# Key, query and weight-split pieces moved from GpSimd to VectorE in a two-layer decoder trunk, with square roots begun one work unit later, query copies two units later, and the first norm begun one unit earlier

## Chip, core and metric

The kernel runs on one core of a Trainium2 chip. The metric is device time in microseconds of one execution. The engines are TensorE (PE, with PEld for its weight loads), VectorE (DVE), ScalarE (ACT), GpSimd (POOL) and SyncE (SP), which starts the transfers of weights.

## What is computed

A decoder of two layers on 256 tokens of width 1024, in float32. Each layer is a gated feed-forward block, a mixer with three attention branches, and a second feed-forward block:

```python
for l in range(DEPTH):                                   # DEPTH = 2
    x = x + 0.5 * swiglu_ffn(x, ffn1_norm[l], ffn1_w_gu[l], ffn1_w_down[l])
    h = rms_norm(x, mix_norm[l])
    x = x + hybrid_mixer(h, ...)
    x = x + 0.5 * swiglu_ffn(x, ffn2_norm[l], ffn2_w_gu[l], ffn2_w_down[l])
...
# hybrid_mixer: one projection h @ w_in, split into the inputs of
#   o_a: stick-breaking attention (4 heads)
#   o_b: NSA attention (8 query heads; compressed, selected and window keys)
#   o_c: DSA attention (4 query heads, an indexer picks the top 64 keys)
merged = g_a * (o_a @ w_br_a) + g_b * (o_b @ w_br_b) + g_c * (o_c @ w_br_c)   # g = sigmoid(h @ w_gate)
return merged @ w_out
# queries and keys: rms_norm over 64 columns, then a rotation (rope) of the first 16
```

## The kernel before

**Units.** All weights pass through `unit` (lines 229 to 247). A unit is one 128x1024 (sometimes 128x896) block of weights: SP loads it into one of four `raw` buffers, ACT copies it, rounded, into one of three `wh` buffers (line 242), and DVE, or for the units that the list `slow` names GpSimd, writes the rest `raw - wh` into `wl` (line 244). Two units later (`LA = 2`) PE multiplies with `wh` and `wl`. So a unit's `raw` buffer is free for the next load only when its `wl` is written, and its `wh` buffer only when PE has used it.

**Threads.** Everything else of the mixer (norms, rope, transposes, the indexer's top-k, attention) is written as generators. `tick` (line 209) runs after every unit and advances each generator to its next `yield`; `yield n` means n units later. A scheduler then sets the order of the instructions on DVE, ACT, GpSimd and SP; each engine runs its own list strictly in that order. PE keeps the written order.

**Where the change is.** In the mixer, `norm_rope` (line 665) squares, sums, takes a root with `head_rsqrt` (line 654: one DVE instruction for `u`, then Ln and Exp on ACT, line 501, then three DVE instructions), scales and calls `rope` (line 640). `keys` treats the DSA queries and all keys (`p1`, 9 heads), `queries` the 8 NSA queries (`q8`, two token tiles), `compress` the compressed keys. `stack_k` (line 695) makes a rounded copy and a rest of keys ("L part", line 700); line 790 does the same for the DSA queries. In `indexer` the top-k is 8 rounds of max (line 757) and match-replace (line 758) for each of the two token tiles. `evac` (lines 526 and 528) empties PSUM accumulators (`acc`, three banks) of the input projection. `u`, `y`, `w` of the roots share small buffers, two of each; the root `N["r"]` of the norm ahead of the mixer (line 398) lies in one of the `y` buffers for the whole projection.

**The first norm.** `first_norm` (line 1175) waits two units after its sums and runs `norm_rstd`, which waits `FY2 = 2` more units between its root (line 388) and the product that spreads it (`tp<-dg`, line 413).

Of the kernel before, what the change touches and what calls it, by code (L numbers as in the profile page):

```python
# [112 lines left out]
WB = 2  # L113
WARM = 46
M0 = 7
FY2 = 2
ACC = 3
SC = 2
TP = 2
# [4 lines left out]
def decoder_trunk(ctx: ExitStack, tc: tile.TileContext, x_in, consts, gains, hgain, gu1, dn1, win, wkc, wgate, cw1, cw2,  # L124
# [17 lines left out]
    def nm(s):  # L142
        cnt[0] += 1
        return f"{s}_{cnt[0]}"
# [37 lines left out]
    def psum(tag, bufs):  # L182
        return ps.tile([P, 512], F32, tag=tag, bufs=bufs, name=nm(tag))
# [203 lines left out]

    def rsqrt(src, n, inv):

        u, y, w = (small.tile([P, 32], F32, tag=t, bufs=2, name=nm(t))[:, 0:n] for t in "uyw")  # L390
        V.tensor_scalar(out=u, in0=src, scalar1=inv, scalar2=EPS, op0=ALU.mult, op1=ALU.add)
        V.tensor_scalar(out=y.bitcast(I32), in0=u.bitcast(I32), scalar1=-0.5, scalar2=float(0x5f3759df), op0=ALU.mult,
                        op1=ALU.add)
        for _ in range(3):
            V.tensor_tensor(out=w, in0=y, in1=y, op=ALU.mult)
            V.scalar_tensor_tensor(out=w, in0=w, scalar=-0.5, in1=u, op0=ALU.mult, op1=ALU.mult)
            V.scalar_tensor_tensor(out=y, in0=w, scalar=1.5, in1=y, op0=ALU.add, op1=ALU.mult)
        return y
# [91 lines left out]
    def mixer(l, nrm, nxt):  # L490
# [9 lines left out]
        def act_exp(func=AF.Exp, **kw):  # L500
            e = A.activation(func=func, **kw)  # L501
            nosync(e, table)
            exps.append(e)
# [4 lines left out]
        def st(shape, tag, bufs, n):  # L508
            return small.tile([P] + shape, F32, tag=tag, bufs=bufs, name=nm(n))
# [26 lines left out]
                yield 1  # L536


        gate, iw = st([NT, 24], "gate", 2, "gate"), st([NT, 8], "iw", 2, "iw")
        rq = st([NT], "rq", 2, "rq")  # L540
        p0 = b4("p0")[:, 0:640].rearrange("p (t c) -> p t c", t=NT)
        vds = mt([NT, HD], "vds")
# [97 lines left out]
        def rope(v, nh, half, cs, sn):  # L640

            nt = cs.shape[1]
            sh = [P, nt, nh, 2 * half]
            a = mt([NT, 9, 16], "ra")[:, 0:nt, 0:nh, 0:2 * half]
            b = mt([NT, 9, 16], "rb")[:, 0:nt, 0:nh, 0:2 * half]
            cb = cs.unsqueeze(2).to_broadcast(sh)
            sb = sn.unsqueeze(2).to_broadcast(sh)
            V.tensor_tensor(out=a, in0=v[:, :, :, 0:2 * half], in1=cb, op=ALU.mult)
            G.tensor_tensor(out=b[:, :, :, 0:half], in0=v[:, :, :, half:2 * half], in1=sb[:, :, :, 0:half], op=ALU.mult)  # L649
            V.tensor_tensor(out=b[:, :, :, half:2 * half], in0=v[:, :, :, 0:half], in1=sb[:, :, :, half:2 * half],  # L650
                            op=ALU.mult)
            V.tensor_tensor(out=v[:, :, :, 0:2 * half], in0=a, in1=b, op=ALU.add)

        def head_rsqrt(ss, n):

            u, y, w = (st([32], t, 2, t)[:, 0:n] for t in "uyw")
            V.tensor_scalar(out=u, in0=ss, scalar1=1.0 / HD, scalar2=EPS, op0=ALU.mult, op1=ALU.add)
            act_exp(out=y, in_=u, func=AF.Ln)
            act_exp(out=y, in_=y, scale=-0.5)
            V.tensor_tensor(out=w, in0=y, in1=y, op=ALU.mult)  # L660
            V.scalar_tensor_tensor(out=w, in0=w, scalar=-0.5, in1=u, op0=ALU.mult, op1=ALU.mult)
            V.scalar_tensor_tensor(out=y, in0=w, scalar=1.5, in1=y, op0=ALU.add, op1=ALU.mult)
            return y

        def norm_rope(v, nh, gs, t0=0):

            nt = v.shape[1]
            ss = st([32], "hs", 2, "hs")[:, 0:nt * nh]
            for t in range(nt):
                sq = b4("sq")[:, 0:nh * HD].rearrange("p (h d) -> p h d", d=HD)  # L670
                A.activation(out=sq, in_=v[:, t], func=AF.Square)
                V.tensor_reduce(out=ss[:, t * nh:(t + 1) * nh], in_=sq, axis=AX.X, op=ALU.add)
            yield 1
            r = head_rsqrt(ss, nt * nh).rearrange("p (a b) -> p a b", b=nh)
            yield 1
            V.tensor_tensor(out=v, in0=v, in1=r.unsqueeze(3).to_broadcast([P, nt, nh, HD]), op=ALU.mult)
            for a, n, k in gs:
                g = hg[:, k * HD:(k + 1) * HD].unsqueeze(1).unsqueeze(1)
                V.tensor_tensor(out=v[:, :, a:a + n], in0=v[:, :, a:a + n], in1=g.to_broadcast([P, nt, n, HD]),  # L679
                                op=ALU.mult)  # L680
            yield 1
            rope(v, nh, 8, tab("cs")[:, t0:t0 + nt], tab("sn")[:, t0:t0 + nt])
            yield 0
# [11 lines left out]
        def stack_k(dst, src, nh):  # L695

            d = dst.rearrange("p h (a d) -> p h a d", d=HD)
            b = src.unsqueeze(2).to_broadcast([P, nh, 2, HD])
            A.activation(out=d[:, :, 0:2].bitcast(F32R), in_=b, func=AF.Copy)
            G.tensor_tensor(out=d[:, :, 2:4], in0=b, in1=d[:, :, 0:2], op=ALU.subtract)  # L700

        live = {"E": EB, "PT": 4}
        later = [cc("ncz")[:, S - P * (t + 1):S] for t in range(NT)]
# [68 lines left out]
        def keys():  # L772
# [14 lines left out]
                evens(out=kD[:, :, s], in_=heads(tp))  # L787
            dq = b4("dq").rearrange("p (t h a d) -> p t h a d", t=NT, a=2, d=HD)
            A.activation(out=dq[:, :, :, 0].bitcast(F32R), in_=p1[:, :, 0:4], func=AF.Copy)
            G.tensor_tensor(out=dq[:, :, :, 1], in0=p1[:, :, 0:4], in1=dq[:, :, :, 0], op=ALU.subtract)  # L790
            done.add("kSW")
            yield 1
            for t in range(NT):
# [9 lines left out]
        def compress():  # L803
# [47 lines left out]
            junk = mt([1, 256], "kc4")[:, 0, 0:HD]  # L851
            css = st([1], "css", 2, "css")
            A.activation(out=junk, in_=kc, func=AF.Square, accum_out=css)
            yield 1
            rc = head_rsqrt(css, 1)
            V.scalar_tensor_tensor(out=kc, in0=kc, scalar=rc, in1=hg[:, 5 * HD:6 * HD], op0=ALU.mult, op1=ALU.mult)
            ra, rb = st([16], "cra", 2, "cra"), st([16], "crb", 2, "crb")
            V.tensor_tensor(out=ra, in0=kc[:, 0:16], in1=cc("csc"), op=ALU.mult)
# [15 lines left out]
        def queries():  # L874
            yield from need(4)
            parts = [norm_rope(q8[t][:, :, HD:P].unsqueeze(1), 8, ((0, 8, 3),), t) for t in range(NT)]
            for _ in zip(*parts):
                yield 1
            for t in range(NT):
                A.activation(out=q8[t][:, :, 0:HD].bitcast(F32R), in_=q8[t][:, :, HD:P], func=AF.Copy)  # L880
                V.tensor_tensor(out=q8[t][:, :, HD:P], in0=q8[t][:, :, HD:P], in1=q8[t][:, :, 0:HD], op=ALU.subtract)
            yield 4
            for t in range(NT):
                for h in range(0, 8, 4):
                    tp = transposes([q8[t][:, h + j] for j in range(4)])
                    evens(out=qN[:, h:h + 4, t * P:(t + 1) * P], in_=heads(tp))
                if t == 0:
                    yield 1
            done.add("qN")
# [48 lines left out]
        def dsa():  # L938
            yield from need("mdsa", "qD")
            for t in range(NT):  # L940
# [9 lines left out]
                PT = attn_pt(t, E)  # L950
                live["E"] += 1
                yield 1
                o = psum("tp", TP)
                for b in range(t + 1):
                    for h in range(4):
                        mm(o[h % 2 * HD:(h % 2 + 1) * HD, h // 2 * P:(h // 2 + 1) * P], vds[:, b], PT[h][b],
# [138 lines left out]
        for g in (keys, indexer, queries, nsa_units, compress, stick_breaking, nsa, compressed, dsa):  # L1095
            spawn(g())
        gates = iter(range(12))
        slow.extend(int(u in (10, 14, 18, 27)) for u in range(62))
        for g in ORDER:
            if g == "f":  # L1100
                for kv in range(2):
# [73 lines left out]
    def first_norm():  # L1175
        for m in range(KD):
# [2 lines left out]
                yield 1  # L1179
            if m == 6:  # L1180
                nc.sync.dma_start(out=cst, in_=consts)
        yield 2
        yield from norm_rstd(nrm, FY2)
        yield 4
        V.tensor_scalar(out=negi, in0=ident, scalar1=NEG, scalar2=None, op0=ALU.mult)
# [81 lines left out]
```

## Time and profile before

| | before |
|---|---|
| median of 3 runs | 1226.95 us (1223.9 to 1229.97) |
| profiled execution: time | 1228.48 us |
| its span | 1226.7 us |
| PE busy | 1206.3 us, 98% |
| PEld busy | 1075.5 us, 88% |
| DVE busy | 886.6 us, 72% |
| ACT busy | 697.6 us, 57% |
| POOL busy | 163.4 us, 13% |

Busy shares are means over the whole span. The two mixers lie about 205 to 440 us and 810 to 1045 us into it; the feed-forward blocks fill the rest.

### The profile page before, as it was taken

What the parts mean: (1) busy time and instruction counts of PE and PEld (TensorE: products, weight loads), DVE (VectorE), ACT (ScalarE), POOL (GpSimd) and SP (SyncE); (2) the same over time, 40 slices, a digit from 0 to 9 for tenths busy, and PEclk for the clock granted to TensorE, in tenths of its full rate; (3) what the DMA queues carried; (4) which work ended last, traced back from release to release, by engine and by line L of the source; (5) the groups of instructions that cost most, each with busy time, mean ns of one, the idle gap of its engine ahead of it and who ended that gap; (6) DMA issues with size and microseconds to landing.
All of it is one profiled execution on the core that took longest, in us unless ns stands there. A gap on an engine that the chain in (4) does not pass through costs nothing.

```text
span 1226.7 us, 20872 instructions
## 1 busy us (share of the span) xinstructions
PE 1206.3 (98%) x7878; PEld 1075.5 (88%) x7878; DVE 886.6 (72%) x1563; ACT 697.6 (57%) x1261; POOL 163.4 (13%) x195
## 2 busy tenths in 40 slices
PE   8999999989999999999999999999999999999998
PEld 7888888878989988888888888897798899888887
DVE  7766677896766877766777766778877578776664
ACT  6655555555666565555556555545556745655542
POOL 2111011330000111110111110122300001111100
PEclk9999999999999999999999999999999999999999
DMA  7555566644334565556656655665433346555563
GB/s 265 178 188 184 179 188 193 213 145 131 106 102 141 177 193 191 191 185 182 189 182 196 191 186 184 191 197 192 139 127 112 104 148 195 181 192 190 186 198 104
DMA packets 60885, 212.09 MB, mean 173 GB/s; under 512 B 6992, under 2 KB 8048, under 8 KB 60784
## 3 DMA queue, kind: packets, MB, share of 16 engines
q1 hardware_dynamic: 60192, 209.65, 53.7%
q0 software_dynamic: 448, 1.08, 0.4%
q8 instruction: 62, 1.02, 0.3%
q14 instruction: 39, 0.32, 0.1%
q10 hardware_dynamic: 144, 0.02, 0.0%
HBM read 209.15 MB, written 1.05 MB: 171 GB/s over the span
## 4 chain that ended last, share of the span: by engine, by line
PE 89%; DVE 6%; DMA 2%; ACT 1%; POOL 1%; issue 1%; SPq 0%; ACTq 0%; DVEq 0%; POOLq 0%
PE acc L196 67%; PE sc L196 17%; PE tp L689 2%; DVE wl L244 2%; PE o L196 1%; DMA raw<-in_win 1%; DVE isc L758 1%; PE tp L196 1%; DVE m L757 1%; ACT wh L242 1%; DVE isc L748 1%; DMA gn<-in_gains 0%; POOL rb L649 0%; DVE p L679 0%; DVE isc L746 0%
## 5 line engine op out<-in xcount | busy, mean ns | idle before, releaser
L242 ACT ACTIVATE wh<-raw 128x1024 fp32r<-128x1024 f32 (+4 forms) x402 | 412.1, 1027 | 412.4 <-PE acc L196 285.6
L244 DVE TENSOR_TENSOR wl<-raw,wh 128x1024 fp32r<-128x1024 f32 (+3 forms) x394 | 468.3, 1191 | 221.5 <-ACT wh L242 220.4
L196 PE MATMUL acc<-aT,wh 128*128 128x512 f32 (+1 forms) x1696 | 414.1, 342 | 1.1 <-ACT wh L242 1.1
L196 PEld LDWEIGHTS acc<-aT,wh 128*128 128x128 f32 x1696 | 264.9, 189 | 41.0 <-ACT wh L242 1.5
L196 PE MATMUL acc<-aT,wl 128*128 128x256 f32 x1280 | 297.1, 280 | 0.7 <-DVE wl L244 0.7
L196 PE MATMUL acc<-hT,wh 128*128 128x512 f32 (+1 forms) x792 | 239.1, 369 | 0.0
L196 PEld LDWEIGHTS acc<-aT,wl 128*128 128x128 f32 x1280 | 215.9, 189 | 3.0 <-DVE wl L244 2.0
L196 PE MATMUL sc<-aT,wh 128*128 128x512 f32 x544 | 190.8, 395 | 0.0
L196 PE MATMUL acc<-hT,wl 128*128 128x256 f32 x704 | 186.6, 283 | 0.0
L196 PEld LDWEIGHTS acc<-hT,wh 128*128 128x128 f32 x792 | 137.4, 188 | 26.9
L196 PE MATMUL sc<-aT,wl 128*128 128x256 f32 x544 | 150.6, 278 | 0.0
L196 PEld LDWEIGHTS acc<-hT,wl 128*128 128x128 f32 x704 | 127.1, 188 | 0.0
L442 POOL TENSOR_TENSOR v<-v,R 128x256 f32<-128x256 f32 x88 | 68.2, 779 | 414.3 <-DVE v L358 359.9
L196 PEld LDWEIGHTS sc<-aT,wh 128*128 128x128 f32 x544 | 101.8, 188 | 23.6
L196 PEld LDWEIGHTS sc<-aT,wl 128*128 128x128 f32 x544 | 102.3, 188 | 0.4
L386 POOL TENSOR_TENSOR ssum<-ssum,sq 128x256 f32<-128x256 f32 x42 | 38.3, 912 | 449.1 <-ACT sq L385 448.9
L196 PE MATMUL acc<-wh,aT 128*128 128x512 f32 (+1 forms) x320 | 83.9, 404 | 4.6 <-ACT p L526 4.6
L196 PEld LDWEIGHTS acc<-wh,aT 128*128 128x128 f32 x320 | 59.3, 194 | 15.9 <-ACT p L526 5.5
L357 ACT ACTIVATE half<-acc 128x256 f32<-128x256 f32 x136 | 49.4, 365 | 2.6 <-PE acc L196 1.8
L444 DVE TENSOR_TENSOR v<-v,v 128x256 f32<-128x256 f32 x88 | 38.4, 440 | 12.1 <-ACT v L443 4.3
L376 DVE SCALAR_TENSOR_TENSOR aT<-x,gn,aT 128x256 fp32r<-128x256 f32 x48 | 40.5, 853 | 6.9 <-ACT aT L375 6.9
L501 ACT ACTIVATE E<-sc,mx 128x128 f32<-128x128 f32 (+1 forms) x80 | 32.6, 418 | 21.8 <-DVE mx L905 21.7
(241 smaller groups left out, 1262.8 us busy)
## 6 DMA issues: line engine op xcount, KB each, us to landing
raw<-in_gu SPq DMA_DIRECT2D x175, 512.0 KB, 3.7
raw<-in_dn SPq DMA_DIRECT2D x64, 512.0 KB, 3.5
raw<-in_wgate SPq DMA_DIRECT2D x48, 512.0 KB, 3.4
raw<-in_win SPq DMA_DIRECT2D x32, 512.0 KB, 3.5
raw<-in_dn SPq DMA_DIRECT2D x32, 384.0 KB, 3.0
raw<-in_wbr SPq DMA_DIRECT2D x16, 512.0 KB, 3.4
raw<-in_wout SPq DMA_DIRECT2D x16, 512.0 KB, 3.5
raw<-in_cw SPq DMA_DIRECT2D x8, 512.0 KB, 4.5
```

What stands on the lines that cost most here:

```text
L196: return pe(T.matmul(o, lhsT=lhsT, rhs=rhs, start=start, stop=stop, skip_group_check=True))
L242: A.activation(out=wh[:, w], in_=raw[:, w], func=AF.Copy)
L244: e.tensor_tensor(out=wl[:, w], in0=raw[:, w], in1=wh[:, w].bitcast(F32), op=ALU.subtract)
L357: A.activation(out=t, in_=b[:, S:2 * S], func=AF.Copy)
L376: V.scalar_tensor_tensor(out=dst[:, m, 1], in0=xs[m], scalar=g[:, m:m + 1], in1=dst[:, m, 0].bitcast(F32), op0=ALU.mult, op1=ALU.subtract)
L386: G.tensor_tensor(out=ssum, in0=ssum, in1=sq, op=ALU.add)
L442: G.tensor_tensor(out=g, in0=g, in1=N["R"], op=ALU.mult)
L444: V.tensor_tensor(out=u, in0=u, in1=g, op=ALU.mult)
L501: e = A.activation(func=func, **kw)
L689: pe(T.transpose(tp[:, b * P:(b + 1) * P], src, ident))
L748: V.scalar_tensor_tensor(out=isc[t], in0=rl[:, j], scalar=w, in1=isc[t], op0=ALU.mult, op1=ALU.add)
L757: V.max(out=m8, in_=isc[t])
```

## The change

Several pieces of the mixer change their engine and keep their arithmetic: the first half of `rope`'s second product (line 649), the L part of the keys (`stack_k`, line 700, five calls per layer), the L part of the DSA queries (line 790), and the `wl` of units 10, 14 and 18 go from GpSimd to DVE; unit 27's `wl` stays on GpSimd. `head_rsqrt` becomes a generator: it writes `u`, yields one unit, and then issues Ln and Exp; the yield that stood ahead of it is gone. The root's buffers become three `u`, four `y` and two `w`, of 18 columns instead of 32. `queries` waits two units ahead of its copies (lines 880 and 881) and two behind them, where it waited none and four. The DSA output bank comes from `acc` instead of `tp`. `first_norm` waits one unit less, `FY2` one more. `gate` and `iw` have one buffer.

```diff
-FY2 = 2
+FY2 = 3
...
     def rsqrt(src, n, inv):
-        u, y, w = (small.tile([P, 32], F32, tag=t, bufs=2, name=nm(t))[:, 0:n] for t in "uyw")
+        u, y, w = (small.tile([P, 18], F32, tag=t, bufs={'u': 3, 'y': 4, 'w': 2}[t], name=nm(t))[:, 0:n] for t in "uyw")
...
-            G.tensor_tensor(out=b[:, :, :, 0:half], in0=v[:, :, :, half:2 * half], in1=sb[:, :, :, 0:half], op=ALU.mult)
+            V.tensor_tensor(out=b[:, :, :, 0:half], in0=v[:, :, :, half:2 * half], in1=sb[:, :, :, 0:half], op=ALU.mult)
...
         def head_rsqrt(ss, n):
-            u, y, w = (st([32], t, 2, t)[:, 0:n] for t in "uyw")
+            u, y, w = (st([18], t, {'u': 3, 'y': 4, 'w': 2}[t], t)[:, 0:n] for t in "uyw")
             V.tensor_scalar(out=u, in0=ss, scalar1=1.0 / HD, scalar2=EPS, op0=ALU.mult, op1=ALU.add)
+            yield 1
             act_exp(out=y, in_=u, func=AF.Ln)
...
         def norm_rope(v, nh, gs, t0=0):
...
-            yield 1
-            r = head_rsqrt(ss, nt * nh).rearrange("p (a b) -> p a b", b=nh)
+            r = (yield from head_rsqrt(ss, nt * nh)).rearrange("p (a b) -> p a b", b=nh)
...
-            G.tensor_tensor(out=d[:, :, 2:4], in0=b, in1=d[:, :, 0:2], op=ALU.subtract)
+            V.tensor_tensor(out=d[:, :, 2:4], in0=b, in1=d[:, :, 0:2], op=ALU.subtract)
...
-            G.tensor_tensor(out=dq[:, :, :, 1], in0=p1[:, :, 0:4], in1=dq[:, :, :, 0], op=ALU.subtract)
+            V.tensor_tensor(out=dq[:, :, :, 1], in0=p1[:, :, 0:4], in1=dq[:, :, :, 0], op=ALU.subtract)
...
             for _ in zip(*parts):
                 yield 1
+            yield 2
             for t in range(NT):
...
-            yield 4
+            yield 2
...
-                o = psum("tp", TP)
+                o = psum("acc", ACC)
...
-        slow.extend(int(u in (10, 14, 18, 27)) for u in range(62))
+        slow.extend(int(u == 27) for u in range(62))
...
-        yield 2
+        yield 1
         yield from norm_rstd(nrm, FY2)
```

The scheduler's lists move with it. On DVE, where the second query tile (`q_403`) is turned and copied in the first mixer, the list before reads as follows (`m_642` is the last of the eight top-k rounds, `mdsa` the mask that they give):

```order
L676 TENSOR_TENSOR q_403_2154<-q_403_2154,y_2870 128x8x64
L652 TENSOR_TENSOR q_402_2153<-ra_2956,rb_2957 128x8x16
L679 TENSOR_TENSOR q_403_2154<-q_403_2154,hg_2139 128x8x64
L244 TENSOR_TENSOR wl_3034<-raw_3031,wh_3033 128x1024
L648 TENSOR_TENSOR ra_2962<-q_403_2154,cst 128x128
L650 TENSOR_TENSOR rb_2963<-q_403_2154,cst 128x8x8
L881 TENSOR_TENSOR q_402_2153<-q_402_2153 128x8x64
L652 TENSOR_TENSOR q_403_2154<-ra_2962,rb_2963 128x8x16
L758 MATCH_REPLACE isc_2376<-m_642_3313,isc_2376 128x256
L763 SCALAR_TENSOR_TENSOR mdsa_3316<-isc_2375,cst 128x128
L244 TENSOR_TENSOR wl_3069<-raw_3066,wh_3068 128x1024
L881 TENSOR_TENSOR q_403_2154<-q_403_2154 128x8x64
```

and now, from the same turn of `q_403` to its copy (`m_587` and `m_588` are the fourth round, `m_598` and `m_599` the fifth):

```order
L652 TENSOR_TENSOR q_403_2154<-ra_2962,rb_2963 128x8x16
L758 MATCH_REPLACE isc_2375<-m_587_2993,isc_2375 128x128
L757 MAX m_588_2996<-isc_2376 128x8
L244 TENSOR_TENSOR wl_3002<-raw_2999,wh_3001 128x1024
L758 MATCH_REPLACE isc_2376<-m_588_2996,isc_2376 128x256
L244 TENSOR_TENSOR wl_3030<-raw_3027,wh_3029 128x1024
L757 MAX m_598_3056<-isc_2375 128x8
L757 MAX m_599_3059<-isc_2376 128x8
L758 MATCH_REPLACE isc_2375<-m_598_3056,isc_2375 128x128
L758 MATCH_REPLACE isc_2376<-m_599_3059,isc_2376 128x256
L881 TENSOR_TENSOR q_402_2153<-q_402_2153 128x8x64
L881 TENSOR_TENSOR q_403_2154<-q_403_2154 128x8x64
```

The query chain now stands ahead of four and a half of the eight top-k rounds and of two unit splits that it stood behind.

On ACT, in the same mixer, the roots (L501, Ln and Exp into `y`) stood one behind the other, between the units' copies (L242) and the evacuations of transposed keys (L784):

```order
L242 ACTIVATE wh_2926<-raw_2924 128x1024
L501 ACTIVATE y_2804<-u_2803 128x1
L501 ACTIVATE y_2804<-y_2804 128x1
L242 ACTIVATE wh_2970<-raw_2968 128x1024
L501 ACTIVATE y_2861<-u_2860 128x8
L784 ACTIVATE kSW_2164<-tp_2944 128x4x128
L501 ACTIVATE y_2861<-y_2861 128x8
L784 ACTIVATE kSW_2164<-tp_2950 128x4x128
L242 ACTIVATE wh_3005<-raw_3003 128x1024
L501 ACTIVATE y_2870<-u_2869 128x8
L699 ACTIVATE kc_564_2878<-c2s_2752 128x128
L501 ACTIVATE y_2870<-y_2870 128x8
```

and now:

```order
L242 ACTIVATE wh_2926<-raw_2924 128x1024
L501 ACTIVATE y_2758<-u_2757 128x1
L501 ACTIVATE y_2804<-u_2803 128x8
L501 ACTIVATE y_2812<-u_2811 128x8
L501 ACTIVATE y_2758<-y_2758 128x1
L501 ACTIVATE y_2804<-y_2804 128x8
L501 ACTIVATE y_2812<-y_2812 128x8
L242 ACTIVATE wh_2970<-raw_2968 128x1024
L784 ACTIVATE kSW_2164<-tp_2944 128x4x128
L784 ACTIVATE kSW_2164<-tp_2950 128x4x128
L242 ACTIVATE wh_3001<-raw_2999 128x1024
L699 ACTIVATE kc_564_2878<-c2s_2752 128x128
```

The three roots (compressed key, two query tiles) stand together, ahead of the evacuations instead of among them.

On DVE, where the keys are turned (`p_401`) and the indexer's second tile begins (`isc_2376`), the list before was:

```order
L679 TENSOR_TENSOR p_401_2152<-p_401_2152,hg_2139 128x2x128 x2
L746 TENSOR_SCALAR isc_2376<-rl_2630,iw_2148 128x256
L648 TENSOR_TENSOR ra_2666<-p_401_2152,cst 128x288
L748 SCALAR_TENSOR_TENSOR isc_2376<-rl_2630,iw_2148,isc_2376 128x256
L650 TENSOR_TENSOR rb_2667<-p_401_2152,cst 128x18x8
L652 TENSOR_TENSOR p_401_2152<-ra_2666,rb_2667 128x18x16
L244 TENSOR_TENSOR wl_2697<-raw_2694,wh_2696 128x1024
```

and now:

```order
L679 TENSOR_TENSOR p_401_2152<-p_401_2152,hg_2139 128x2x128 x2
L746 TENSOR_SCALAR isc_2376<-rl_2630,iw_2148 128x256
L244 TENSOR_TENSOR wl_2649<-raw_2646,wh_2648 128x1024
L748 SCALAR_TENSOR_TENSOR isc_2376<-rl_2630,iw_2148,isc_2376 128x256
L648 TENSOR_TENSOR ra_2666<-p_401_2152,cst 128x288
L649 TENSOR_TENSOR rb_2667<-p_401_2152,cst 128x18x8
L650 TENSOR_TENSOR rb_2667<-p_401_2152,cst 128x18x8
L244 TENSOR_TENSOR wl_2697<-raw_2694,wh_2696 128x1024
L652 TENSOR_TENSOR p_401_2152<-ra_2666,rb_2667 128x18x16
```

Unit 14's split (`wl_2649`) and the rope product (L649) have joined DVE's list here.

## Rows read from the trace of the kernel before

**Rows 1.** Page, busy time of engines: us, share of the span, instructions.

```profile
PE 1206.3 (98%) x7878; PEld 1075.5 (88%) x7878; DVE 886.6 (72%) x1563; ACT 697.6 (57%) x1261; POOL 163.4 (13%) x195
```

**Rows 2.** Windows: length, busy PE, PEld, DVE, ACT, POOL, PE clock, DMA share, GB/s.

```profile
240.00:260.00 20.00, 18.08 (x110) 15.61 (x110) 19.78 (x51) 12.59 (x24) 10.24 (x9) 1.00 0.46 152
260.00:285.00 25.00, 21.18 (x96) 16.35 (x96) 20.07 (x58) 12.51 (x25) 4.11 (x4) 0.93 0.46 148
...
845.00:865.00 20.00, 18.12 (x106) 15.80 (x106) 19.78 (x52) 13.22 (x24) 9.04 (x8) 0.91 0.51 167
865.00:890.00 25.00, 22.05 (x102) 17.11 (x100) 20.23 (x58) 12.47 (x26) 5.78 (x5) 0.93 0.44 138
```

**Rows 3.** The same windows view of three shorter stretches.

```profile
275.00:285.00 10.00, 8.07 (x32) 6.59 (x33) 5.08 (x9) 5.29 (x9) 0.16 (x1) 0.83 0.50 160
...
850.00:855.00 5.00, 4.81 (x16) 3.91 (x17) 4.95 (x11) 3.54 (x7) 1.88 (x2) 0.66 0.32 105
...
880.00:885.00 5.00, 2.69 (x8) 1.97 (x7) 3.57 (x9) 2.72 (x7) 0.79 (x1) 0.73 0.55 167
```

**Rows 4.** Waits of PE: instruction, releaser, us in total, times, longest us.

```profile
PE acc L196 <- ACT p L526: 4.6, 2, 2.3
...
PE tp L689 <- ACT PT L929: 1.5, 2, 0.7
...
PE tp L196 <- DVE dg L409: 1.0, 1, 1.0
```

**Rows 5.** Timeline of PE: start, length, instructions, idle time before and its releaser.

```profile
276.93 1.94 PE L196 MATMUL acc<-wh,aT 128*128 128x512 f32 x6 [2.31 <-ACT p L526]
```

**Rows 6.** Timeline of ACT in the first mixer.

```profile
265.16 0.21 ACT L501 ACTIVATE y<-u 128x8 f32<-128x8 f32 x1 [3.44 <-DVE c2s L856]
...
273.46 1.06 ACT L242 ACTIVATE wh<-raw 128x1024 fp32r<-128x1024 f32 x1
275.52 0.63 ACT L880 ACTIVATE q<-q 128x512 fp32r<-128x512 f32 x1 [1.01 <-DVE q L652]
276.06 0.46 ACT L526 ACTIVATE p<-acc,rq 128x256 f32<-128x256 f32 x1
```

**Rows 7.** Timeline of POOL in the first mixer.

```profile
223.16 2.42 POOL L244 TENSOR_TENSOR wl<-raw,wh 128x1024 fp32r<-128x1024 f32 x1
...
238.70 2.64 POOL L244 TENSOR_TENSOR wl<-raw,wh 128x1024 fp32r<-128x1024 f32 x1 [13.12 <-ACT wh L242]
...
259.23 1.91 POOL L866 TENSOR_TENSOR p<-c2s,cst 128x512 f32<-128x512 f32 x1
...
273.05 2.11 POOL L649 TENSOR_TENSOR rb<-q,cst 128x64 f32<-128x64 f32 x1 [2.92 <-DVE q L679]
```

**Rows 8.** Timeline of DVE in the first mixer.

```profile
223.38 2.35 DVE L748 SCALAR_TENSOR_TENSOR isc<-rl,iw,isc 128x128 f32<-128x128 f32 x1
...
232.74 1.23 DVE L244 TENSOR_TENSOR wl<-raw,wh 128x1024 fp32r<-128x1024 f32 x1 [1.67 <-ACT wh L242]
...
239.14 2.35 DVE L746 TENSOR_SCALAR isc<-rl,iw 128x256 f32<-128x256 f32 x1
...
251.75 0.42 DVE L757 MAX8 m<-isc 128x8 f32<-128x256 f32 x1
...
275.20 0.29 DVE L652 TENSOR_TENSOR q<-ra,rb 128x128 f32<-128x128 f32 x1 [0.21 <-POOL rb L649]
```

**Rows 9.** DVE groups from 205 to 300 us: busy us, mean ns, idle before.

```profile
L244 DVE TENSOR_TENSOR wl<-raw,wh 128x1024 fp32r<-128x1024 f32 x18 | 22.2, 1232 | 6.7 <-ACT wh L242 6.6
...
L724 DVE TENSOR_TENSOR q<-p,q 128x512 f32<-128x512 f32 x2 | 1.4, 688 | 0.0
...
L718 DVE TENSOR_TENSOR ik<-p,ik 128x128 f32<-128x128 f32 x1 | 0.3, 284 | 0.0
```

**Rows 10.** Chain that ended last, one top-k round: start, us, what.

```profile
253.93 0.52 DVE m L757 x2
254.45 0.66 DVE isc L758 x2
```

More of the change, by code (lines that the diff above doesn't have):

```diff
@@ L536, in need @@
                 yield 1
-        gate, iw = st([NT, 24], "gate", 2, "gate"), st([NT, 8], "iw", 2, "iw")
+        gate, iw = st([NT, 24], "gate", 1, "gate"), st([NT, 8], "iw", 1, "iw")
         rq = st([NT], "rq", 2, "rq")
@@ L667, in norm_rope @@
             nt = v.shape[1]
-            ss = st([32], "hs", 2, "hs")[:, 0:nt * nh]
+            ss = st([18], "hs", 2, "hs")[:, 0:nt * nh]
             for t in range(nt):
@@ L853, in compress @@
             A.activation(out=junk, in_=kc, func=AF.Square, accum_out=css)
-            yield 1
-            rc = head_rsqrt(css, 1)
+            rc = yield from head_rsqrt(css, 1)
             V.scalar_tensor_tensor(out=kc, in0=kc, scalar=rc, in1=hg[:, 5 * HD:6 * HD], op0=ALU.mult, op1=ALU.mult)
```

## Prediction

> **What bounds the kernel now.** I read the page's engine totals first, then the windows view in stretches, then what PE waits for, and last the timelines of the engines that it waits for. PE is busy 1206.3 of 1226.7 us [rows 1], so almost all of the time is matmuls that the change does not touch, and the most that any such change can give back is PE's idle time and the time in which PE runs below its full clock. The windows put most of it in one place of each mixer. From 240 to 285 us PE lacks 1.92 and 3.82 us of being fully busy, from 845 to 890 us 1.88 and 2.95 us, together 10.57 us, while DVE is busy 19.78 of 20 us there: DVE is the engine that PE follows in these two stretches [rows 2]. Behind the longer stalls the granted clock is below 1.00: 0.83, 0.66 and 0.73 in three stretches; busy time times what is missing is 0.17 x 8.07 + 0.34 x 4.81 + 0.27 x 2.69 = 3.74 us [rows 3]. Smaller pieces are two waits of 1.5 us together for the transposed attention weights, and 1.0 us in the opening for the spread norm (`dg`) [rows 4]. In sum 10.57 + 3.74 + 1.5 + 1.0 = 16.8 us can be had at most.
>
> The largest single wait is for the evacuation of `acc` on ACT, 2.3 us in each mixer [rows 4], at 276.93 us in the first [rows 5]. ACT shows why: the evacuation (L526, 276.06) stands behind the copy of the second query tile (L880, 275.52), which waited for DVE to turn that tile [rows 6], and DVE's turn waited for GpSimd's rope product, 2.11 us for 64 columns [rows 7, 8]. So the chain is DVE's queue, GpSimd, DVE, ACT, PE.
>
> **The move to DVE.** Thirteen instructions per layer join DVE: three 1024-wide splits at 1.232 us, three 512-wide L parts (two of keys, one of DSA queries) at 0.688, and seven small ones (three 128-wide L parts, four rope products), each at most the 0.284 of a 128-wide tensor_tensor: 3.70 + 2.06 + 1.99 = 7.75 us, an upper bound [rows 9]. Against it stands DVE time that was no work. While GpSimd ran its split from 223.16 to 225.58 us, a 128-wide DVE instruction that started at 223.38 took 2.35 us and ended at 225.73; while GpSimd ran the next split to 241.34, a 256-wide one from 239.14 took 2.35 us too [rows 7, 8]. Clean ones take 0.28 at 128 and, between the 0.284 at 128 and the 0.688 at 512 columns, about 0.42 at 256 [rows 9], so the two lost 2.07 and 1.93 us. I therefore take it that the two engines shut each other out, and that this part of DVE's busy time goes with the GpSimd splits. The bounds of what DVE's queue gains per layer are 7.75 (no collision returned) and 7.75 - 4.0 - 0.21 = 3.5 us (these two and the wait for the rope product [rows 8] returned); I take the lower one, since start and end of the long instructions lie that close to GpSimd's.
>
> Up to 251.75 us it comes out even: two splits, one 512-wide and three small pieces add 2.46 + 0.69 + 0.85 = 4.0, and 4.0 come back. GpSimd's slow split also held a `raw` buffer until 225.58, the next load could start only then, and DVE stood idle 1.67 us at 232.74 for a copy that waited for data [rows 7, 8]. With the split done on DVE some 3 us earlier that idle time goes: DVE reaches the place of 251.75 about 1.7 us earlier.
>
> **Roots and query copies.** From 251.75 to 275.20, when DVE turned the second query tile, DVE needed 23.45 us [rows 8]. By the order, four and a half top-k rounds of 0.52 + 0.66 = 1.18 us [rows 10] now stand behind that turn, minus 5.3; one split fewer stands ahead of it, minus 1.2; two 512-wide and four small pieces join, plus 2.5; the wait for GpSimd goes, minus 0.2. That leaves 19.25 us, or 271.0 on the old clock, 269.3 with the 1.7 us from above. PE wants the evacuation at 276.93 - 2.31 = 274.6 [rows 5]. Without its earlier stalls, 1.92 to 260 us and 3.82 - 2.31 = 1.51 behind it [rows 2, 5], it wants it at 271.2. The margin is 1.9 us, and it decides the case. The three roots no longer share one free `y` buffer: ACT stood 3.44 us until DVE had used the old root (`c2s`, L856), with key evacuations behind it [rows 6]. That wait goes; the roots cost the same instructions as before. The new yield issues Ln a unit after `u`. Queued behind it on ACT are the next unit's copy and the key evacuations, for which PE waits; with `u` a unit old, the wait ahead of them should be nil.
>
> **What stays.** Per layer: (1) ACT has one unit's copy, 1.06 us, and two evacuations of 0.46 us between PE's end of a unit and its next bank; the copy started at 273.46, so without L880 the bank would be free at 275.4 instead of 276.9, 0.8 us after PE wants it [rows 5, 6]: 0.7 stay, rounded for overlap. (2) Top-k rounds and splits pushed behind the query copies (three splits, three rounds, masks and a cast, about 3.7 + 3.5 + 1.3 = 8.5 us [rows 9, 10]) stand ahead of the second cast of transposed queries; counted from the copies' end that is about 0.9 us later than PE wants it. (3) GpSimd's `vpad` product (L866, 1.91 us [rows 7]) stays, and now falls between DVE's query pieces; at worst DVE waits all of it, and the compressed key's transpose, which has no slack, waits too: 1.9. Together 3.5, or 7.0 us for both layers, between 0 (all hidden) and 7.0 as I take them.
>
> **The small edits.** The root of the first norm starts one unit earlier and its product keeps its unit, so `dg` is ready and the 1.0 us go [rows 4]; some of its tiny DVE instructions now stand ahead of a split. I count them as hidden, since a split is made two units ahead of its use; without that cover eight of them at no more than 0.284 us [rows 9] would cost 2.3. With the DSA output in `acc`, both `tp` banks are free for transposes, and the 1.5 us [rows 4] go; if `acc` is short instead, the same 1.5 stay. Fewer and narrower buffers elsewhere cost nothing: `gate` and `iw` of the second layer are written 600 us after the first's last use.
>
> **Sum.** 16.8 - 7.0 = 9.8 us. The profiled execution took 1228.48 us, 1.5 above the median of the runs; taken off the median, 1226.95 - 9.8 gives 1217. The runs of before spread over 6 us, so 0.5% (6.1 us) is about what can be told from no change.
>
> **A rule against it.** The windows show DVE full where the work is added [rows 2]. The Trainium skill, Perfetto Trace Analysis, section Optimizing Scalar/DVE Operations, says that with DVE saturated it may make sense to offload work to ScalarE or even GpSimd; this change does the reverse. The same section adds that the two share an SBUF port, so that moving work between them might not help; the long instructions above bear out the second half, and the first, taken alone, would give the slower rival below: 1236 by it, 1217 by the rows.
>
> **Rivals.**
> Slower: DVE's long instructions are not GpSimd's doing but waits that the view does not show, so nothing is returned. Then each layer has 7.75 us more on the engine that PE follows, less the 2.1 us of GpSimd's rope product: 2 x 5.6 less the 2.5 of the small edits is 8.8, so 1236. For it: DVE at 19.78 of 20. Against: ends that agree within 0.15 us, twice. It decides if DVE turns the second query tile later than 275 on the old clock. Chance 0.10.
> The stall stays: DVE is more than 1.9 us later than my sum, from waits for copies or transfers. Then 4.6 us of stalls and their clock (1.37 + 0.73) are kept, and 9.8 - 6.7 + 1.4 (item 1, counted twice) = 4.5 are won: 1222.5. For it: a margin of 1.9 in a sum of 19; against: the 3.44 us wait that also goes. Chance 0.20.
> All of it: nothing of the 7.0 stays, 1210. For it: (3) needs the worst meeting; against: (1) is plain in the rows. Chance 0.08.
> No change: the top-k pushed back makes the DSA mask late, and its wait eats the gain, 1227. Against: DVE has room behind 278 us, busy 5.08 of 10 [rows 3]. Chance 0.04.
> My forecast: 0.58, with 1213 to 1221 as its own range.
>
> **How the numbers follow.** Faster by over 0.5% (below 1220.8): nearly all of the forecast, the largest gain and a little of the second rival, 0.66. Slower: the first rival, 0.10. Within: the rest, 0.24. The range leaves out the slower rival and the far half of the largest gain: 1211.5 to 1226.
>
> **What would show it.** In the changed kernel's profile: PE idle from 240 to 285 and from 845 to 890 us below 4 us per layer instead of 5, and the clock at 1.00 there; no DVE instruction of the indexer above 1 us; DVE busy about 7 us higher in total, POOL lower by 14 us or more (two splits and the last rope product are 7.2 us per layer [rows 7]); the `acc` wait for L526 below 1 us each; `dg` and PT gone from PE's waits. It would be wrong if PE's waits named `wl` or transposes of `kc` or `q` for over 2 us per layer, or the clock fell again behind a new stall.

## Result and the profile after

The changed kernel takes 1212.6 us (median of four runs, 1210.1 to 1216.6) against 1228.1 us for the kernel before beside it: ratio 0.988, 95% interval 0.984 to 0.992. A second set of runs gave 1210.2 against 1225.7 us, ratio 0.988 (0.986 to 0.990). The forecast was 1217 us. The profiled execution took 1214.88 us, 13.6 less than that of before; the rows below are of it. Its mean granted clock is 0.995, that of the profiled execution of before 0.996.

The page's engine totals, to be held against [rows 1]:

```profile
PE 1202.2 (99%) x7878; PEld 1075.1 (89%) x7878; DVE 889.0 (73%) x1589; ACT 698.4 (58%) x1261; POOL 132.5 (11%) x169
```

PE is busy 4.1 us less, DVE 2.4 us more, GpSimd 30.9 us less. The windows of [rows 2]:

```profile
240.00:260.00 20.00, 20.00 (x124) 17.83 (x123) 19.38 (x60) 13.99 (x29) 1.05 (x1) 1.00 0.47 148
260.00:285.00 25.00, 23.23 (x120) 19.23 (x119) 22.88 (x59) 11.88 (x19) 2.35 (x1) 0.96 0.50 164
845.00:865.00 20.00, 20.00 (x125) 17.66 (x124) 20.00 (x65) 14.11 (x30) 1.05 (x1) 1.00 0.50 157
865.00:890.00 25.00, 23.24 (x121) 19.65 (x120) 20.86 (x55) 10.97 (x21) 2.35 (x1) 0.86 0.39 128
```

PE's idle time in the two stretches falls from 10.57 to 1.77 + 1.76 = 3.53 us, all of it now in the second window of each. The waits of PE name it; of those of [rows 4] none is left:

```profile
PE sc L196 <- DVE qN L637: 3.3, 2, 1.6
PE acc L196 <- DVE wl L244: 1.4, 3, 0.6
```

PE now waits once in each mixer for the second cast of the transposed queries (`qN`). PE's timeline there, and DVE's and POOL's:

```profile
281.24 0.62 PE L196 MATMUL sc<-kC,qN 128*128 128x32 f32 x4 [1.64 <-DVE qN L637]
281.71 2.84 PE L196 MATMUL acc<-wh,aT 128*128 128x512 f32 x8
284.35 1.91 PE L196 MATMUL acc<-wl,aT 128*128 128x512 f32 x4
286.06 1.11 PE L689 MATMUL tp<-cst,p 128*128 128x128 f32 x8
```

```profile
264.69 0.27 DVE L652 TENSOR_TENSOR q<-ra,rb 128x128 f32<-128x128 f32 x1
...
278.05 2.54 DVE L763 SCALAR_TENSOR_TENSOR mdsa<-isc,cst 128x128 bf16<-128x128 f32 x2
280.51 0.68 DVE L637 CAST qN<-tp 128x512 fp32r<-128x512 f32 x1
```

```profile
277.75 2.35 POOL L244 TENSOR_TENSOR wl<-raw,wh 128x1024 fp32r<-128x1024 f32 x1 [21.01 <-ACT wh L242]
```

The query turn (L652) is at 264.69 instead of 275.20 us [rows 8]. The mask instructions (L763) ahead of the cast take 2.54 us while GpSimd makes unit 27's split, the only split left on it from 277.75 to 280.10. Behind PE's wait twelve matmuls take 4.35 us (281.71 to 286.06). The clock of the window is 0.96; in the second mixer, behind the same wait, it is 0.86, and from 882 to 886 us PE runs all the time at 0.50, the lower of its two levels (1.2 of 2.4 GHz):

```profile
882.00:886.00 4.00, 4.00 (x11) 3.13 (x10) 1.27 (x5) 1.20 (x2) 0.00 (x0) 0.50 0.00 0
```

### The profile page after: what moved, and what is told of

The parts are those of the page before. It is cut to its first block, busy times and chain, and to the rows that moved or that the text cites. A ratio compares the mean times of both kernels' runs of the same rounds, so it can differ in the third digit from the quotient of the medians.

```text
span 1213.1 us, 20854 instructions
## 1 busy us (share of the span) xinstructions
PE 1202.2 (99%) x7878; PEld 1075.1 (89%) x7878; DVE 889.0 (73%) x1589; ACT 698.4 (58%) x1261; POOL 132.5 (11%) x169
## 3 DMA queue, kind: packets, MB, share of 16 engines
HBM read 209.15 MB, written 1.05 MB: 173 GB/s over the span
## 4 chain that ended last, share of the span: by engine, by line
PE 96%; DVE 2%; ACT 1%; DMA 1%; issue 0%; POOL 0%; SPq 0%; POOLq 0%
PE acc L196 74%; PE sc L196 17%; PE tp L689 2%; PE o L196 2%; DMA x<-in_x 1%; DVE wl L244 1%; PE tp L196 0%; DVE mdsa L763 0%; ACT wh L242 0%; DVE isc L758 0%; DVE qN L637 0%; DVE m L757 0%; ACT aT L375 0%; ACT p L526 0%; SPq L168 0%
## 5 line engine op out<-in xcount | busy, mean ns | idle before, releaser
L242 ACT ACTIVATE wh<-raw 128x1024 fp32r<-128x1024 f32 (+4 forms) x402 | 412.3, 1028 | 410.9 <-PE acc L196 285.0
L244 DVE TENSOR_TENSOR wl<-raw,wh 128x1024 fp32r<-128x1024 f32 (+4 forms) x400 | 474.0, 1187 | 210.9 <-ACT wh L242 209.9
L196 PE MATMUL acc<-hT,wh 128*128 128x512 f32 (+1 forms) x792 | 236.2, 367 | 0.0
L358 DVE TENSOR_TENSOR v<-acc,half 128x256 f32<-128x256 f32 x108 | 44.7, 417 | 1.5 <-ACT half L357 1.5
L501 ACT ACTIVATE E<-sc,mx 128x128 f32<-128x128 f32 (+1 forms) x80 | 32.6, 419 | 21.9 <-DVE mx L905 21.8
```

Of the source, the lines that this page charges most:

```text
L196: return pe(T.matmul(o, lhsT=lhsT, rhs=rhs, start=start, stop=stop, skip_group_check=True))
L242: A.activation(out=wh[:, w], in_=raw[:, w], func=AF.Copy)
L244: e.tensor_tensor(out=wl[:, w], in0=raw[:, w], in1=wh[:, w].bitcast(F32), op=ALU.subtract)
L358: V.tensor_tensor(out=o, in0=b[:, 0:S], in1=t, op=ALU.add)
```

## Experiments

The first theory, T1, is that of the prediction: GpSimd and DVE shut each other out, and the query turn moved ahead of top-k rounds is what frees PE. Its rivals are that the moves alone, or the order alone, do it, or that DVE is so full that moves cost. Each kernel was timed against the kernel before; the four of one batch share a chip. The kernel before had medians of 1226.7, 1225.7 and 1226.1 us in the three batches, so kernels of different batches are compared by their gains, that is, by what each takes less than the kernel before beside it.

**First batch.** One split more, and the change in pieces.

```
e1: after,  slow.extend(0 for u in range(62))        # was int(u == 27)
e2: before, slow.extend(int(u == 27) for u in range(62))
e3: e2, and V for G at L649 (rope), L700 and L790 (L parts)
e4: after, with G again at those lines and splits 10, 14, 18, 27 on G
```

e1: 

> The changed kernel with unit 27's split on DVE too, so that no split is left on GpSimd. Theory 1 (a GpSimd tensor_tensor and DVE shut each other out): the DVE instruction of 2.54 us at 278.05 shrinks to about 0.7, the second query cast is some 1.8 us earlier, the wait of 1.64 us for qN at 281.24 goes, and with it the slow clock behind it (12 matmuls 4.35 instead of 2.82 us): 2 x (1.6 + 1.5) = 6.2 us less, 1206 to 1209 us. Rival (DVE is the bound of this stretch): DVE has 1.23 us more to do ahead of the cast, PE waits longer, 1214 to 1216 us. Rival (wl of unit 27 itself is what comes late, or nothing is bound there): 1211 to 1214 us.

e2: 

> The kernel before with one thing changed: the splits of units 10, 14 and 18 on DVE; rope, L parts, roots and query copies as before. Theory 1: collisions and the late raw buffer go (4.0 and 1.7 us of DVE's time per layer against 3.7 added), but the query turn still stands behind the top-k; L652 of the second query tile about 2 to 3 us earlier than 275.2 and the acc wait for L526 shorter by as much: 1220 to 1224 us. Rival (the splits are all that matters): 1212 to 1216 us, as the whole change. Rival (only order matters, the move costs or does nothing): 1226 to 1232 us.

e3: 

> The kernel before with all thirteen instructions per layer moved to DVE, roots, buffers and query copies as before. Theory 1: like the splits alone, with 4.0 us more DVE work per layer and the rope waits for GpSimd gone, query turn still behind the top-k: L652 at 273 to 275, 1221 to 1225 us. Rival (the moves are the whole gain): 1212 to 1216 us. Rival (DVE is full, so moves cost): 1230 to 1240 us.

e4: 

> The changed kernel with all engine moves undone (splits 10, 14, 18, rope product and L parts on GpSimd again): only roots, buffers, query copies, first norm and DSA bank are new. Theory 1: the long DVE instructions and the wait of 1.67 us for the late load are back, but four and a half top-k rounds (5.3 us) are out of the query chain and the roots do not wait: L652 at about 270 on the clock of before, wait for L526 mostly gone; waits of 240 to 260 us kept: 1218 to 1222 us. Rival (order is the whole gain, the moves do nothing): 1212 to 1215 us. Rival (order does nothing without the moves): 1225 to 1230 us.

Measured: e1 1209.4 us, ratio 0.985 (0.984 to 0.987); e2 1220.3, 0.994 (0.993 to 0.996); e3 1210.5, 0.987 (0.985 to 0.988); e4 1219.1, 0.993 (0.992 to 0.995). e2 and e4 fell in T1's ranges, e1 just above its own. e2 did so for another reason than T1's: its wait for L526 is 4.6 us as before, and what went are the waits of 3.5 us for the indexer's `rl` and of 0.9 us for `kSW`. e3 was far off: the moves alone give 16 us, as much as the whole change, though roots and query copies are as before. What differs is the order of DVE's queue, which the scheduler sets when the kernel is built. Counted in the built queues, the top-k maxima (two to a round, 16 in a mixer) that stand ahead of the second query's turn, beside its time on the first mixer's timeline:

```
kernel             maxima ahead   L652 of the second query, us
before                  16              275.20
e4 order only           14              267.19
e2 splits only          13              271.80
e3 moves only            8              269.28
after, e1                7              264.69, 264.73
```

Not all of these differences are the turn's: the last matmul ahead of the mixer ends at 197.0 us in before and e2, 197.2 in e3, 195.7 in after and e1 and 193.8 in e4.

With more work in DVE's queue the scheduler put four top-k rounds further back, which I had counted under roots and query copies. Those alone (e4) move one round; they bring the turn forward by making the two query tiles' chains one piece, so that two splits of 1.21 us that stood ahead of the turn stand behind it. So the moves (2.1 us of it left in e3) and the order edits (none left in e4) each shorten the same wait for L526 in their own way, and the gains don't add. e4 paid elsewhere, as the waits of PE in it show:

```profile
PE tp L689 <- DVE kD L637: 5.9, 2, 3.0
PE sc L196 <- ACT rl L742: 3.1, 3, 1.6
```

The acc wait is gone, but a key cast (`kD`) on DVE is now late by 3.0 us in each mixer, and the wait for the indexer's `rl` is there, as it is in e9 below, the other kernel with the three splits on GpSimd.

In e1 the wait for `qN` was 0.9 us in each mixer, not 0: the split, 1.23 us, now stands on DVE ahead of the cast, which I had left out of the expectation. The masks of e1, with nothing on GpSimd beside them:

```profile
278.08 0.62 DVE L763 SCALAR_TENSOR_TENSOR mdsa<-isc,cst 128x128 bf16<-128x128 f32 x2
278.61 1.23 DVE L244 TENSOR_TENSOR wl<-raw,wh 128x1024 fp32r<-128x1024 f32 x1
```

**Second batch.** A repeat; moves without roots and copies; the collision by itself; a better place for the cast.

```
e0: after, unchanged
e5: e3, slow empty, FY2 = 3, first norm one unit earlier, DSA o in psum("acc", ACC)
e6: e1, and for unit 27, behind DVE's split:
+   G.tensor_tensor(out=idle[0], in0=raw[:, w], in1=wh[:, w].bitcast(F32), op=ALU.subtract)
    # idle[0] is the tile fk, whose last reader is L814
e8: e1, and at the qN copies
-   evens(out=qN[:, h:h + 4, t * P:(t + 1) * P], in_=heads(tp))
+   A.activation(out=qN[:, h:h + 4, t * P:(t + 1) * P], in_=heads(tp), func=AF.Copy)
```

e0: 

> The changed kernel once more, beside the next three on one chip. Its first runs were 1210.1 and 1210.4 us at a granted clock of 1.0 and 1214.9 and 1216.6 us at 0.995 and 0.994. Theory (the wait of 1.64 us for qN in each mixer drops the clock behind it in some executions and not in others): the runs fall into these two groups again, 1210 to 1217 us. Rival (the first runs were disturbed): all at 1210 to 1211 us.

e5: 

> The kernel before with the thirteen moved instructions, unit 27's split on DVE too, the first norm's root a unit earlier and the DSA output in acc; roots, their buffers and query copies as before. The moves alone gave 1210.5 us, with waits of 1.5 us for PT and 0.9 us for dg left in them. Theory 1 (these two waits go, and roots and later query copies give nothing beside the moves): 1207 to 1209 us. Rival (roots and query copies are needed once the rest is gone): 1210 to 1213 us, with the acc wait for L526 of 1.1 us per mixer or more.

e6: 

> The changed kernel with unit 27's split on DVE, and a second copy of the same product on GpSimd into a tile that nobody reads any more, so that GpSimd works at the same moment but nothing waits for it. Theory 1 (running beside DVE is what costs): the mdsa instruction of L763 (two of 0.6 us together without GpSimd) takes about 2.5 us again, DVE's split comes behind it, PE's wait for qN is 2.5 to 3 us instead of 0.9: 1213 to 1219 us. Rival (the wait came from data that GpSimd made late): as with the split on DVE alone, 1208 to 1210 us, and L763 takes 0.6 us.

e8: 

> The changed kernel with unit 27's split on DVE and all four casts of the transposed queries on ACT, where two of them were on DVE behind that split; ACT is idle from 278.6 us there. Theory 1 (the cast's place in DVE's queue is what PE waits for): the last cast ends at about 279.3 instead of 280.4 us, the waits of 0.9 us for qN go: 2 x 0.9 us less than with the split on DVE alone (1209.4), 1207 to 1208 us. Rival (what comes next, kC or the masks, is late by as much): 1209 to 1210 us.

Measured: e0 1210.2 us, 0.988 (0.986 to 0.990); e5 1209.4, 0.986 (0.985 to 0.988); e6 1217.1, 0.993 (0.991 to 0.995); e8 1205.9, 0.983 (0.981 to 0.985).

e5 lies between its two ranges: roots and copies are as before, L526 is still waited for, 1.1 us in one mixer and 0.6 in the other, and it gains 16.3 us where e1 gained 17.4.

e6 settles the collision. Nobody reads what GpSimd makes there, yet DVE's instruction is long again. POOL's, DVE's (line numbers are 3 higher here) and PE's rows of e6:

```profile
276.10 2.35 POOL L246 TENSOR_TENSOR fk<-raw,wh 128x1024 f32<-128x1024 f32 x1 [20.90 <-ACT wh L242]
```

```profile
276.18 0.41 DVE L761 MATCH_REPLACE8 isc<-m,isc 128x256 f32<-128x256 f32 x1
276.50 2.43 DVE L766 SCALAR_TENSOR_TENSOR mdsa<-isc,cst 128x128 bf16<-128x128 f32 x2
278.86 1.21 DVE L244 TENSOR_TENSOR wl<-raw,wh 128x1024 fp32r<-128x1024 f32 x1
279.99 0.68 DVE L640 CAST qN<-tp 128x512 fp32r<-128x512 f32 x1
```

```profile
PE sc L196 <- DVE qN L640: 5.7, 2, 2.8
```

The pair of mask instructions takes 2.43 us beside GpSimd and, in e1, 0.62 without it. The price of one useless GpSimd product per layer is 1217.1 - 1209.4 = 7.7 us between the medians (8.8 between the gains), of which 5.7 - 1.8 = 3.9 are PE's longer waits (1.8 in e1). The rest I put to the clock, 0.994 to 0.996 in all of e6's runs and 0.996 to 1.0 in e1's; in the profiled executions it is 0.89 from 260 to 285 us and 0.66 from 880 to 890 in e6, 1.00 in both in e1.

e8 is the fastest. The row of ACT where the last casts now stand, and PE's rows behind them:

```profile
276.49 1.09 ACT L886 ACTIVATE qN<-tp 128x512 fp32r<-128x512 f32 x2 [0.28 <-PE tp L689]
```

```profile
276.64 1.94 PE L196 MATMUL sc<-kC,qN 128*128 128x32 f32 x16
278.43 2.09 PE L196 MATMUL acc<-wh,aT 128*128 128x512 f32 x8
280.35 1.07 PE L196 MATMUL acc<-wl,aT 128*128 128x512 f32 x4
281.26 1.03 PE L689 MATMUL tp<-cst,p 128*128 128x128 f32 x8
```

PE runs through without a wait, and the same twelve matmuls take 281.26 - 278.43 = 2.83 us. At 1205.9 us it lies below its range of 1207 to 1208; between the gains it is 19.8 - 17.4 = 2.4 us better than e1, where 1.8 were expected.

e0's five runs spread as the first four had. Of the nine, five lie at 1208.5 to 1210.4 us with a mean granted clock of 0.997 to 1.0, four at 1213.1 to 1216.6 with 0.994 to 0.997: behind the same wait the clock falls in some executions and not in others. The second mixer, first in the execution of after shown above, then in e0's, which stays at full clock there:

```profile
880.13 1.04 PE L196 MATMUL sc<-kC,qN 128*128 128x32 f32 x4 [1.63 <-DVE qN L637]
881.00 3.76 PE L196 MATMUL acc<-wh,aT 128*128 128x512 f32 x8
884.56 1.91 PE L196 MATMUL acc<-wl,aT 128*128 128x512 f32 x4
```

```profile
878.52 0.62 PE L196 MATMUL sc<-kC,qN 128*128 128x32 f32 x4 [1.64 <-DVE qN L637]
878.98 2.07 PE L196 MATMUL acc<-wh,aT 128*128 128x512 f32 x8
880.89 1.07 PE L196 MATMUL acc<-wl,aT 128*128 128x512 f32 x4
```

From start to end the twelve matmuls take 5.47 us in the one and 2.98 in the other.

**Third batch.** T3, formed from the table: the top-k rounds ahead of the query turn decide. Two kernels change that order with no instruction moved for it, one turns it back.

```
e9: before, and in the top-k loop (turned[True] is L652 of the second query, once written)
-   V.max(out=m8, in_=isc[t])
+   mx8 = V.max(out=m8, in_=isc[t])
+   if True in turned: nosync(mx8, turned[True])     # order on DVE alone
e10: e2 with the same edit
e11: e3, and between top-k rounds yield 1            # was 2
e12: e8 without the root buffers, the roots' yield and the later query copies
```

e9: 

> The kernel before, with no instruction moved to another engine: only the order of DVE's queue is changed, by holding each top-k round that is written after the second query tile's turn (L652) behind it. Six top-k maxima instead of 16 then stand ahead of that turn, five rounds of 1.18 us. Theory 3 (what matters in all these kernels is how many top-k rounds stand ahead of the query turn): L652 at about 269.5 instead of 275.2 us, the two acc waits of 2.3 us for L526 and the slow clock behind them go: 1216 to 1220 us. Rival (the collisions with GpSimd are the cause, the order only follows): 1224 to 1228 us.

e10: 

> The kernel before with splits 10, 14 and 18 on DVE (1220.3 us by itself) and the same hold; rope product, L parts, roots and query copies as before. Six maxima instead of 13 ahead of the query turn. Theory 3: L652 at about 267.5 instead of 271.8 us, and with it what the rope and L parts on DVE gave (13 maxima to 8): 1209 to 1213 us. Rival (rope and L parts gain by leaving GpSimd, not by the order): 1218 to 1221 us.

e11: 

> The kernel before with all thirteen instructions moved (1210.5 us by itself), and the top-k rounds written one unit apart instead of two, so that 12 maxima stand ahead of the query turn instead of 8. Theory 3: two rounds, 2.4 us, are back in the chain, L652 at about 271.6 instead of 269.3 us, the wait for L526 2 to 3 us per mixer instead of 1.1, and the slow clock behind it: 1214 to 1219 us. Rival (the moves gain whatever the order): 1209 to 1212 us.

e12: 

> The fastest kernel so far (all on DVE, casts of the transposed queries on ACT, 1205.9 us) with the change's root buffers, the yield in the roots and the later query copies undone; the first norm and the DSA bank stay. Theory (roots and query copies give nothing beside the moves): 1205 to 1207 us. Rival (they hide the evacuation behind the query copies): waits of about 1 us for L526 in each mixer, 1208 to 1211 us.

Measured: e9 1218.2 us, 0.993 (0.991 to 0.995); e10 1210.7, 0.987 (0.986 to 0.989); e11 1221.8, 0.997 (0.995 to 0.998); e12 1208.9, 0.986 (0.984 to 0.987).

The waits of PE in e9, then in e10:

```profile
PE sc L196 <- ACT rl L742: 3.4, 3, 1.7
PE acc L196 <- ACT p L526: 2.0, 2, 1.0
```

```profile
PE acc L196 <- ACT p L526: 2.2, 2, 1.2
```

The turn came at 270.93 us in e9 and 266.96 in e10, six maxima ahead of it in both. The order alone halves the wait for L526 (4.6 to 2.0) and is worth 7.9 us; the three splits alone 6.4 (e2); both together 15.4 (e10), nearly as much as all thirteen moves (16.2, e3) and as much as the whole change (15.5). So rope and L parts on DVE are worth 9.8 us beside the splits (e2 to e3), but the order without them, one edit, gives 15.4 - 6.4 = 9.0: T3 and not its rival. What the splits remove is the wait for `rl`: 3.4 us in e9, none in e10.

e11 lost as T3 said, 11.3 us against e3 (12.0 between the gains) and more than its range, but not where I had put it. Its query turn was early, 267.13 us. The waits of PE and the row of DVE say what was late:

```profile
PE tp L689 <- DVE dq L790: 7.9, 2, 4.4
```

```profile
266.53 0.70 DVE L790 TENSOR_TENSOR dq<-p,dq 128x512 f32<-128x512 f32 x1
```

The L part of the DSA queries, at 256.74 us in e3, stood ten microseconds later behind top-k rounds, and PE waited 3.5 and 4.4 us to transpose it. T3 holds as "top-k ahead of what PE waits for next", not as "ahead of L652". It also shows the price of the move: an L part on DVE stands in that queue.

e12 fell in its rival's range: without roots and query copies the fastest kernel loses 3.0 us (2.6 between the gains; the intervals overlap a little), and L526 is waited for again, 0.6 us in each mixer:

```profile
PE acc L196 <- ACT p L526: 1.2, 2, 0.6
```

But the rival's cause is the smaller part. From the last matmul ahead of a mixer to the first of its output projection the profiled executions take 203.36 and 202.83 us in e12, 203.10 and 202.45 in e8, 0.6 us between them in sum. Beside the plain moves roots and query copies gave nothing there: 203.64 and 203.74 us in e5, 203.80 and 203.76 in e1.

**Outside the mixers.** Some 2 us between the profiled executions of e12 and e8 lie in matmuls that wait for nothing. `hT` is what the second product of a feed-forward block reads, `mT` what the mixer's output projection reads. PE's busy time with `hT` in one block, before and after:

```profile
720.00:810.00 90.00, 62.05 (x374) 1.00 0.60 190
720.00:810.00 90.00, 61.31 (x374) 1.00 0.61 189
```

and with `mT` in one mixer, before and after:

```profile
408.00:433.00 25.00, 23.20 (x192) 1.00 0.59 188
401.00:426.00 25.00, 22.56 (x192) 1.00 0.60 189
```

The counts are the same and the clock is 1.00, yet the matmuls are shorter. The other way goes the first product of the second layer's first feed-forward block; its groups in that block, before and after:

```profile
L196 PE MATMUL acc<-aT,wl 128*128 128x256 f32 x216 | 59.9, 277 | 0.0
L196 PE MATMUL acc<-aT,wl 128*128 128x256 f32 x216 | 60.6, 281 | 0.0
```

Between the `hT` matmuls of the two blocks around it lie 122.84 us before and 124.99 after. In sum, over four feed-forward blocks and two mixers, 4 x 0.75 + 2 x 0.63 - 2.15 = 2.1 us are won. All fourteen profiled executions fall into two groups by these numbers: `hT` takes 245.2 us in all four blocks together in after, e0, e1, e4, e6 and e8, and 248.2 to 248.3 in before, e2, e3, e5 and e9 to e12. Only the six have the new buffers (the roots', and one for `gate` and `iw`), the roots' yield and the later query copies, and the last two do nothing in these places. That leaves the buffers, by a shift of what lies behind them in memory perhaps; the reason is not shown.

## Why the prediction was right, and where it was not

**Direction, mechanism, range.** Right: both parts of the mechanism are shown, the collisions by e6 and the query turn by e9, though not with the sizes forecast, and 1212.6 us lies in 1211.5 to 1226, a little below the likeliest case's own range. The faster case was given 0.66. Of the signs named, PE's idle time (1.8 us per layer), GpSimd's busy time (30.9 us less) and the waits came out; the clock at 1.00, no indexer instruction of DVE above 1 us and DVE busy 7 us more did not (0.96 and 0.86; masks of 2.54 us a pair; 2.4 us). One sign of being wrong, the clock falling again behind a new stall, came too.

**The sum.** 13.6 us came between the two profiled executions where 9.8 were forecast, but not by the terms of the sum, and that they lie this near is partly luck. Idle time in the mixers gave 10.57 - 3.53 = 7.0, PT 1.5, `dg` 1.0, and PE's busy time fell by 4.1. These 4.1 look like the 3.74 for the clock and are not: missing clock times busy time in the four windows is 0.07 x 21.18 + 0.09 x 18.12 + 0.07 x 22.05 = 4.7 us before [rows 2] and 0.04 x 23.23 + 0.14 x 23.24 = 4.2 after, so the clock gave back about 0.5 at most. 2.1 are the matmuls outside the mixers, which the prediction put at nothing ("Fewer and narrower buffers elsewhere cost nothing"); the other 1.5 no row here assigns. Two terms failed in opposite directions: "What stays", 7.0 us forecast and 3.5 of idle time left, and the clock, all of it counted as returned.

Of "What stays", (1) and (3) were nothing: no wait for L526 is left, and the `vpad` product took 1.05 us and stretched one small DVE instruction by 0.4 (0.55 us at 256.20 for 0.15). (2), the second cast, was 1.6 us per layer, not 0.9, and for another reason: not the rounds pushed behind the copies but unit 27's split on GpSimd, which I had not set against DVE's instructions of that moment (e1, e6).

**The collisions.** Right, by e6. What DVE's queue gained: 2.4 us in all against 7.0 forecast, so per layer up to 7.75 - 1.2 = 6.5 us came back (7.75 was an upper bound) and not 4.2, more than the two cases I had counted. The slower rival, that the long instructions were not GpSimd's doing, falls. The Trainium skill, SBUF — State Buffer, section SBUF: two separate sides, says that a GpSimd instruction that reads SBUF and a DVE instruction with two SBUF inputs, or one in a mode that takes two ports, lock a shared port pair against each other for the whole instruction. The masks with their two inputs agree, 2.43 us against 0.62; so do the maxima with one input, which kept their length in the kernel before while GpSimd made a split. The number of inputs alone does not decide: the indexer's L746 reads one tensor and a scalar and took 2.35 us beside a split [rows 8]; in which mode it ran no row tells. POOL's row and the maxima's:

```profile
252.00 2.42 POOL L244 TENSOR_TENSOR wl<-raw,wh 128x1024 fp32r<-128x1024 f32 x1 [5.78 <-ACT wh L242]
```

```profile
252.67 0.61 DVE L757 MAX8 m<-isc 128x8 f32<-128x128 f32 x2
253.85 0.61 DVE L757 MAX8 m<-isc 128x8 f32<-128x128 f32 x2
```

The Trainium skill, Perfetto Trace Analysis, section Optimizing Scalar/DVE Operations: of the two halves of its advice the first, to offload a saturated DVE, speaks for the kernel before, and taking three splits back gained 6.4 us (e2).

**The query turn.** It was said to decide the case; it was worth about half. e9, which changes only the order around it, gains 7.9 us, and e2 gains 6.4 with the wait for L526 untouched, where the wait for `rl`, which the prediction did not name, is gone. The turn came at 264.69, not 269.3. DVE reached the place of 251.75 at 247.08, 4.7 us earlier instead of 1.7, of which 1.4 are the earlier start of the whole mixer (195.65 for 197.03 us); from there to the turn took 17.6 us instead of 19.25. The count of rounds was right, 16 maxima to 7. What I put them down to was not: the moves alone give 16 to 8, roots and copies alone 16 to 14. The ACT wait of 3.44 us for a `y` buffer did not need new buffers: e10 keeps the old ones, ACT waits 0.76 and 1.51 us ahead of its roots, and e10 gains as much as the change.

**The clock.** I counted all of it as returned. In four of nine runs it was not: in the profiled one twelve matmuls behind the wait of 1.64 us cost 4.35 - 2.83 = 1.5 us more than in e8 in the first mixer, and 5.47 - 2.98 = 2.5 more than in e0 in the second.

**The small edits.** Right: PT and `dg` are gone from the waits in every kernel with them (e4, e5) and stay at 1.5 and about 1.0 us in those without (e2, e9, e10). What each is worth in time was not run by itself.

**What stays open.** Why the buffers change the length of matmuls, where the 1.5 us of PE's busy time lie, what in the scheduler pushes the rounds back, and which part of what DVE gained ahead of 251.75 each collision gave.

## What to carry to other kernels

When work moves onto a full engine, compare the order of the built queue before costing the instructions: here the added work pushed top-k rounds behind the pieces that PE was waiting for, and an order edit of a few lines gave 9.0 us where the work on DVE gave 9.8 (e10 and e3 against e2). Set every instruction that stays on GpSimd against what DVE runs at that moment and at the new times; one leftover split made PE wait 1.6 us in each layer, with its 1.23 us on DVE instead 0.9. Once DVE's queue is the path, the last short piece on it may go to an idle ACT: that made 1205.9 us, the fastest kernel here. Before a busy time that fell is put to the clock, hold the same matmuls against each other in stages that the change does not touch.

## What the runs showed of the hardware

A GpSimd product that nothing reads costs 7.7 us in two layers, through DVE (e6 against e1). Two kinds of DVE instruction ran beside GpSimd at their own length: the maxima above, and in e3 a cast from PSUM, while GpSimd made a split. POOL's row and DVE's:

```profile
280.22 2.54 POOL L244 TENSOR_TENSOR wl<-raw,wh 128x1024 fp32r<-128x1024 f32 x1 [21.67 <-ACT wh L242]
```

```profile
280.81 0.69 DVE L637 CAST qN<-tp 128x512 fp32r<-128x512 f32 x1 [0.28 <-PE tp L689]
```

So a GpSimd instruction costs by what it meets: the same split cost a wait of 1.64 us in the changed kernel and none in e3, where it met that cast. And the same matmul, at a clock of 1.00 and with no wait, took 277 ns on average before and 281 after; the fourteen profiles divide by the small buffers, and why is open.
